# Which projections of a decoder layer run as classical fill and which by seven products: branch B's gates and branch A's u change places

## The chip, the core and the metric

The kernel runs on one core of a Trainium2 chip. Five engines with their own instruction streams share the core's SBUF: TensorE (PE, with its weight loads PEld), VectorE (DVE), ScalarE (ACT), GpSimd (POOL) and SyncE (SP), which here issues most DMA transfers. The metric is the device time of one execution in microseconds (us).

## The reference

Two layers of a decoder trunk on 1024 tokens of width 1024. Each layer projects the normalised input once and feeds three token mixers from slices of the projection:

```python
h = rms_norm(x, g_pre)
p = h @ w_in
(u_a, v_a, gate_a, q_b, k_b, v_b, gate_b, q_c, k_c, v_c, gate_c, merge_logits) = split(p)
y_a = chunk_gmlp(u_a, v_a, gm_w_s, gm_b_s, gm_norm_gain) * silu(gate_a)       # u * (tril(W) LN(v) + b) per 128 tokens
y_b = sliding_window_attention(rope(q_b), rope(k_b), v_b, sinks) * silu(gate_b)  # 8 heads of 64, window 128
y_c = stick_breaking_attention(q_c, k_c, v_c) * silu(gate_c)                    # 4 heads of 128, causal
gates = sigmoid(merge_logits + b_merge)
merged = gates[0] * (y_a @ w_branch_a) + gates[1] * (y_b @ w_branch_b) + gates[2] * (y_c @ w_branch_c)
x = x + rms_norm(merged @ w_out, g_post)
```

All of it is float32. The slices u_a, v_a, gate_a, q_b, gate_b and so on have 512 columns each, k_b and v_b 128, the merge logits 3072.

## The kernel before

**Products in three passes.** Every operand of a matmul is split into a rounded part (`hi`, made by ScalarE) and the rest (`lo`, made by VectorE): `split`, lines 111 and 112. A product is then three matmuls per 128 rows of depth (`mm3`, lines 128 to 130). Since all products go through these helpers, the profile names them by the lines of the helpers and by their tiles.

**Two ways to project.** A slice of the projection is made in one of two ways.
- *Classical fill*: `queue_layer` puts jobs in a queue (`stream`). `proj_t` makes 128 columns with the tokens along the free axis, `proj_n` makes 256 columns with the tokens on partitions. `fill(us)` and `need(label)` take steps of these jobs and put them between the matmuls of the attention branches, so that TensorE has work while other engines make softmaxes. A job's weights are loaded and split one job ahead, into a ring of six tiles (`whi`, `wlo`, `wop`: tag `w`) behind a ring of two raw tiles (`wr`).
- *Seven products*: `dense` takes pairs of 128-column blocks and makes each 2 x 2 block product of halves with seven products in place of eight (Strassen's scheme). It needs sums of quarters of the input, T1, T2, T3 and T4. `Combine` makes these: it loads quarters of the saved input (`hT`), subtracts them on VectorE (lines 694, 698, 700 and 705) and splits them; T1, T2 and T4 take twelve of the 27 SBUF slots (`s0` to `s26`) of 128 x 1024, T3 overwrites half of the input (`place_t3`). `S["T"].go(spare)` does as many of its six steps as free slots allow.

**Order in a layer.** Branch C, branch B, `dense`, `merges`, `project_out`. Branch B works in eight units v, two for each of four query blocks of 128 columns. A unit has `scores` (line 488 on TensorE, then copies and a softmax), two transposes (line 521) and two `attend` (line 545). `scores(v + 2)` is called ahead of unit v's transposes. A query block is projected (`qb`), evacuated by ScalarE (line 279), turned by `rope` (four transfers in SyncE's queue, two passes of GpSimd, lines 293 and 294, one of VectorE, line 295), and split by ScalarE (346) and VectorE (347). Masks of the attention weights are made by GpSimd (line 528).

**The order of the fill around the change** is that of the last line of `queue_layer`: two query blocks, half of v, the other two query blocks, the other half of v, then u. The gates of branch A's first half are fill too; the gates of C and B and the second half of A's gates are pairs of `dense`, as are the merge gates.

**Branch A** is done inside `dense`: statistics of v (lines 617 and 618) and its normalisation (623), the transposed mixing weights (627), and then for each of four groups a product with v and a multiplication with u (640 and 643). The dictionary `then` says behind which pair's third product each piece stands. `gate_task` multiplies one 128-row block of a branch's output with its SiLU gate; the tasks are done at the ends of pairs.

**Who sets the order.** TensorE's order is the one in which the program is written. On the other engines and in the DMA queues a scheduler orders the instructions, and each engine then takes its own in that order.

Of the kernel before, what the change touches and what calls it, by code (L numbers as in the profile page):

```python
# [22 lines left out]
P = 128  # L23
# [4 lines left out]
HT = T // 2  # L28
EPS = 1e-6
NEG = -1e30  # L30
O_UA, O_VA, O_GA = 0, 512, 1024
O_QB, O_KB, O_VB, O_GB = 1536, 2048, 2176, 2304
O_QC, O_KC, O_VC, O_GC = 2816, 3328, 3840, 4352
# [8 lines left out]
def trunk(ctx, tc, x, w_in, gm_w_s, gm_b_s, gm_g, sinks, w_ba, w_bb, w_bc, b_merge, w_out,  # L42
          g_pre, g_post, cos_t, sin_t, out):
    nc = tc.nc
    L = w_in.shape[0]
    x = x.rearrange("b t d -> (b t) d")
    out = out.rearrange("b t d -> (b t) d")
# [12 lines left out]
    def new(dt=F32):  # L60
        i = free.popleft()
        t = sp.tile([P, 1024], dt, name=f"s{i}", tag=f"s{i}", bufs=1)
        held[id(t)] = (i, t)
        return t

    def done(*ts):
        for t in ts:
            free.append(held.pop(id(t))[0])
# [72 lines left out]
    def step():  # L141

        while stream:
            j = stream[0]
            if j.gen is None:
                if j.w is None:
                    j.w = j.load()
                j.gen = j.run(j.w)
                if len(stream) > 1:
                    stream[1].w = stream[1].load()  # L150
            c = next(j.gen, None)
            if c is not None:
                for d in list(deferred):
                    d[0] -= c
                    if d[0] <= 0:
                        deferred.remove(d)
                        d[1]()
                return c
            finished.add(j.label)
            stream.popleft()  # L160
        return None

    def fill(us):
        while us > 0:
            c = step()
            if c is None:
                return
            us -= c

    def need(label):  # L170
        while label not in finished:
            assert step() is not None, label

    def proj_t(label, l, col, evac):

        def run(w):
            wh, wl = w
            for hf in range(2):
                acc = pj()
                for k in range(KD):  # L180
                    mm3(acc, (wh[:, k], wl[:, k]), (h[hf][0][:, k], h[hf][1][:, k]), k == 0, k == KD - 1)
                    if k < KD - 1:
                        yield 0.64
                with tc.high_priority():
                    evac(hf, acc)
                yield 0.64
        stream.append(Job(label, lambda: load_w(w_in[l, :, col:col + P], KD, P), run))
# [57 lines left out]
    def queue_layer(l, S):  # L245
# [104 lines left out]
        def va(j):  # L350
            def ev(pr, acc):
                if j == 0:
                    S["va", pr] = new()
                nc.vector.tensor_copy(S["va", pr].rearrange("p (a b) -> p a b", a=2)[:, :, j * 256:(j + 1) * 256],
                                      acc.rearrange("p (a b) -> p a b", a=2))
            proj_n(f"va{j}", l, O_VA + j * 256, ev)

        def ua(c):
            def ev(hf, acc):
                if hf == 0:  # L360
                    S["ua", c] = new()
                nc.scalar.copy(S["ua", c][:, hf * HT:(hf + 1) * HT], acc)
            proj_t(f"ua{c}", l, O_UA + c * P, ev)
        def qb(hp):
            raw(("qb", hp), O_QB + hp * P, 0.125, lambda: after_q(hp))

        vcj(0); qk(0); qk(1); vcj(1); qk(2); qk(3); gate("a", 0); gate("a", 1)
        raw("kb", O_KB, 1.0, after_k)
        raw("vb", O_VB, 1.0, after_v)
        qb(0); qb(1); va(0); qb(2); qb(3); va(1); ua(0); ua(1); ua(2); ua(3)  # L370

    def branch_c(l, S):
        U = 4 * NB
# [99 lines left out]
    def branch_b(l, S):  # L473
# [86 lines left out]
                nc.sync.dma_start(S["ob"][hp * P:(hp + 1) * P, :], o)  # L560
                done(o)

        need(("qb", 1))
        fill(4)
        ready = {0: scores(0)}
        fill(3)
        ready[1] = scores(1)
# [2 lines left out]
        for v in range(8):  # L570
            if v % 2 == 0:
                o = new()
# [137 lines left out]
    def gate_task(S, br, c):  # L710

        o, g = new(), new()
        nc.sync.dma_start(o, S["o" + br][c * P:(c + 1) * P, :])
        nc.sync.dma_start(g, S["g" + br][c * P:(c + 1) * P, :])
        nc.vector.tensor_tensor(o, o, g, op=ALU.mult)
        nc.scalar.activation(g, g, AF.Sigmoid)
        nc.vector.tensor_tensor(o, o, g, op=ALU.mult)
        nc.sync.dma_start(S["y" + br][c * P:(c + 1) * P, :], o)
        done(o, g)

    def dense(l, S):

        T = S["T"].T
        pairs = [(o + c * P, "g", (br, c)) for o, br, c in ((O_GC, "c", 0), (O_GC, "c", 2), (O_GB, "b", 0), (O_GB, "b", 2),
                                                            (O_GA, "a", 2))]
        pairs += [(O_M + "abc".index(br) * D + dm * P, "m", (i, br, dm)) for i, br in enumerate("cba")
                  for dm in range(0, KD, 2)]

# [76 lines left out]
        a = branch_a(l, S)  # L805
        with tc.issue_after(S["b_act"].ins), tc.issue_after(S["b_dve"].ins):
            next(a)
        tasks = deque([lambda br=br, c=c: gate_task(S, br, c) for br in "cba" for c in range(4)])
        then = {0: lambda: next(a), 1: lambda: (next(a), next(a)), 2: lambda: (next(a), next(a))}
        for p, (col, kind, what) in enumerate(pairs):  # L810
            n = 7 * p
            begin(p + 1)
            u = new()
            out = [new(), new()]
            u2, u3 = u[:, :512], u[:, 512:]
            c11, c12, c21, c22 = (t[:, j * 512:(j + 1) * 512] for t in out for j in range(2))

            def add(o, x, b):
                with tc.high_priority():
                    nc.vector.tensor_tensor(o, x, b, op=ALU.add)  # L820
            p1 = prod(n, "B11")
            if p == len(pairs) - 1:
                S["first"] = load_y(S, "c", True)
            with tc.high_priority():
                nc.scalar.copy(c12, p1)
            add(c11, c12, prod(n + 1, "B21"))
            add(u2, c12, prod(n + 2, "T2"))
            if p in then:
                then[p]()
            add(u3, u2, prod(n + 3, "T3"))  # L830
            p5 = prod(n + 4, "T1")
            add(c22, u3, p5)
            add(u2, u2, p5)
            add(c21, u3, prod(n + 5, "T4"))
            add(c12, u2, prod(n + 6, "B22"))
            done(u)
            for j in range(2):
                if kind == "g":
                    br, c = what
                    nc.sync.dma_start(S["g" + br][(c + j) * P:(c + j + 1) * P, :], out[j])  # L840
                else:
                    i, br, dm = what
                    nc.scalar.activation(out[j], out[j], AF.Sigmoid, bias=bmv(l, "abc".index(br), dm + j))
                    nc.scalar.dma_start(S["sg"][(i * KD + dm + j) * P:(i * KD + dm + j + 1) * P, :], out[j])
            done(*out)
            if p >= 3 and tasks:
                tasks.popleft()()
                if p % 2 and tasks:
                    tasks.popleft()()
        assert not tasks  # L850
        for t in T.values():
            for q in t:
# [232 lines left out]
    with tc.manual_schedule(engines={mybir.EngineType.PE}):  # L1085
# [3 lines left out]
        for l in range(L):  # L1089
            S = states[l]  # L1090
# [49 lines left out]
```

## Time and profile before

| | us |
|---|---|
| median of 3 runs | 2087.54 |
| lowest and highest | 2086.88, 2090.14 |
| the profiled execution | 2087.81 |
| its span, first to last instruction | 2086.1 |
| TensorE busy | 2015.0 |
| VectorE, ScalarE, GpSimd busy | 1218.3, 815.9, 496.5 |

The mean granted clock of TensorE is 0.986 of full speed. Layer 0 takes about the first half of the span. Its branch B runs from 307 us, its seven products from 471 us; those of layer 1 lie about 1031 us later. In the profile `s`, `pj`, `pz`, `ptr` and `pav` are an SBUF slot and the four kinds of PSUM tiles; "a <- b: x, n, m" in a list of waits means that a waited for b, x us in total, n times, the longest m.

### The profile page before, as it was taken

How to read it: one execution, taken by the hardware profiler on the slowest of the kernel's cores; microseconds unless marked ns; L12 is line 12 of the kernel's file. 1: busy time of each engine (PE TensorE's matmuls, PEld its weight loads, DVE VectorE, ACT ScalarE, POOL GpSimd, SP SyncE). 2: the span in 40 equal slices, each digit the busy share in tenths (PEclk: the TensorE clock that was granted, in tenths of full speed). 3: DMA queues.
4: the chain of work that ended last, by engine and by line, in shares of the span. 5: the costliest groups of instructions: out<-in, count | busy, mean ns of one | idle time of the engine just before them, and what ended most of it. 6: DMA issues, size and time to landing. Idle time of an engine off the chain costs nothing.

```text
span 2086.1 us, 26587 instructions
## 1 busy us (share of the span) xinstructions
PE 2015.0 (97%) x10193; PEld 1689.0 (81%) x10193; DVE 1218.3 (58%) x1601; ACT 815.9 (39%) x1485; POOL 496.5 (24%) x501
## 2 busy tenths in 40 slices
PE   7999998998999999999999999989999999999998
PEld 7898887886888888888898888879778888888886
DVE  5555646558776556554546565556677765556533
ACT  6444435543234334213444344445423443432221
POOL 0222222232432230151002221222334222202500
PEclk9999999999999999999999999989999999999999
DMA  7111232123766427633431112222336663376213
GB/s 240 34 41 41 81 82 61 41 73 109 260 235 234 139 80 261 222 133 91 135 129 31 41 41 91 61 61 64 108 129 245 239 214 112 119 254 222 81 51 131
DMA packets 169054, 261.81 MB, mean 126 GB/s; under 512 B 8616, under 2 KB 122336, under 8 KB 168928
## 3 DMA queue, kind: packets, MB, share of 16 engines
q1 hardware_dynamic: 162016, 234.95, 34.3%
q10 hardware_dynamic: 6912, 25.17, 3.0%
q8 instruction: 80, 1.31, 0.3%
q14 instruction: 46, 0.38, 0.1%
HBM read 175.15 MB, written 79.69 MB: 122 GB/s over the span
## 4 chain that ended last, share of the span: by engine, by line
PE 87%; DVE 4%; issue 3%; ACT 2%; POOL 2%; DMA 1%; SPq 0%; POOLq 0%; DVEq 0%; ACTq 0%
PE pj L129 16%; PE pj L128 16%; PE pj L130 16%; PE pz L129 5%; PE pz L130 5%; PE pz L128 5%; PE ptr L129 5%; PE ptr L130 5%; PE ptr L128 5%; PE pz L488 2%; PE ptr L415 1%; PE pav L129 1%; PE pav L545 1%; PE pav L130 1%; POOL s L396 1%
## 5 line engine op out<-in xcount | busy, mean ns | idle before, releaser
L128 PE MATMUL pj<-h,whi 128*128 128x512 f32 x700 | 285.3, 408 | 0.0
L129 PE MATMUL pj<-h,whi 128*128 128x512 f32 x700 | 277.3, 396 | 0.0
L130 PE MATMUL pj<-h,wlo 128*128 128x512 f32 x700 | 276.9, 396 | 0.0
L130 PEld LDWEIGHTS pj<-h,wlo 128*128 128x128 f32 x700 | 131.7, 188 | 31.5
L128 PEld LDWEIGHTS pj<-h,whi 128*128 128x128 f32 x700 | 132.3, 189 | 24.4
L112 DVE TENSOR_TENSOR wlo<-wr,whi 128x1024 fp32r<-128x1024 f32 x80 | 107.0, 1341 | 75.9 <-ACT whi L111 75.5
L129 PEld LDWEIGHTS pj<-h,whi 128*128 128x128 f32 x700 | 132.2, 189 | 22.9
L128 PE MATMUL pj<-whi,h 128*128 128x256 f32 x512 | 149.0, 291 | 1.0 <-ACT h L111 1.0
L111 ACT CAST whi<-wr 128x1024 fp32r<-128x1024 f32 x80 | 84.1, 1051 | 163.0 <-PE pj L129 109.3
L130 PE MATMUL pj<-whi,h 128*128 128x256 f32 x512 | 145.2, 284 | 1.7 <-DVE h L112 1.7
L129 PE MATMUL pj<-wlo,h 128*128 128x256 f32 x512 | 144.8, 283 | 0.0
L111 ACT CAST wop<-s 128x512 fp32r<-128x512 f32 x118 | 73.2, 620 | 183.0 <-PE pz L130 60.7
L111 ACT CAST wop<-wr 128x512 fp32r<-128x512 f32 x120 | 74.4, 620 | 154.2 <-PE ptr L130 38.7
L941 POOL TENSOR_TENSOR s<-s,s 128x512 f32<-128x512 f32 x56 | 81.3, 1455 | 222.1 <-DVE s L935 196.1
L398 DVE TENSOR_TENSOR_SCAN s<-s,ones 128x128 f32<-128x128 f32 (+3 forms) x64 | 87.7, 1370 | 63.7 <-POOL s L393 63.7
L112 DVE TENSOR_TENSOR wop<-wr,wop 128x512 fp32r<-128x512 f32 x120 | 99.8, 836 | 31.9 <-ACT wop L111 31.3
L112 DVE TENSOR_TENSOR wop<-s,wop 128x512 fp32r<-128x512 f32 x118 | 107.3, 909 | 16.3 <-ACT wop L111 16.0
L112 DVE TENSOR_TENSOR s<-ptr,s 128x512 fp32r<-128x512 f32 (+2 forms) x132 | 77.3, 589 | 64.9 <-ACT s L111 64.4
L129 PE MATMUL pj<-h,s 128*128 128x512 f32 x256 | 102.0, 398 | 0.0
L128 PE MATMUL pj<-h,s 128*128 128x512 f32 x256 | 101.2, 395 | 0.0
L130 PE MATMUL pj<-h,s 128*128 128x512 f32 x256 | 100.6, 393 | 0.0
L130 PEld LDWEIGHTS pj<-whi,h 128*128 128x128 f32 x512 | 98.0, 191 | 2.6 <-DVE h L112 2.6
(231 smaller groups left out, 5158.9 us busy)
## 6 DMA issues: line engine op xcount, KB each, us to landing
wr<-in_w_in_dram SPq DMA_DIRECT2D x96, 512.0 KB, 4.2
sg<-s ACTq DMA_DIRECT2D x48, 512.0 KB, 5.0
s<-sg SPq DMA_DIRECT2D x48, 512.0 KB, 5.0
s<-in_w_in_dram SPq DMA_DIRECT2D x28, 512.0 KB, 5.2
s<-in_x_dram SPq DMA_DIRECT2D x16, 512.0 KB, 4.0
hT<-s SPq DMA_DIRECT2D x16, 512.0 KB, 3.4
s<-hT SPq DMA_DIRECT2D x16, 512.0 KB, 4.7
wor<-in_w_out_dram SPq DMA_DIRECT2D x16, 512.0 KB, 3.7
```

The costliest lines, as they stand in the source:

```text
L111: nc.scalar.copy(hi, raw)
L112: nc.vector.tensor_tensor(lo, raw, hi.bitcast(F32), op=ALU.subtract)
L128: nc.tensor.matmul(acc, lh, rh, start=first, stop=False)
L129: nc.tensor.matmul(acc, lh, rl, start=False, stop=False)
L130: nc.tensor.matmul(acc, ll, rh, start=False, stop=last)
L396: nc.gpsimd.affine_select(t2[:, dg], t2[:, dg], pattern=[[-1, P]], compare_op=ALU.is_gt, fill=0.0, base=0, channel_multiplier=1)
L398: nc.vector.tensor_tensor_scan(t1[:, :kl][:, ::-1], t1[:, :kl][:, ::-1], ones.to_broadcast([P, kl]), 1.0, op0=ALU.mult, op1=ALU.mult)
L415: nc.tensor.transpose(pt[:, b - b0], t2[:, b * P:(b + 1) * P], ident)
L488: nc.tensor.matmul(z[:, e * 2 + j], qT[e][:, n * P:(n + 1) * P], kk[i][:, k0:k0 + 256], start=i == 0, stop=i == 1)
L545: nc.tensor.matmul(av[:, j], w, t.rearrange("p (e j) k -> p e j k", j=2)[:, :, j], start=i == 0, stop=i == len(ops) - 1)
L941: eng.tensor_tensor(acc[dm][:, ts], acc[dm][:, ts], sg[:, ts], op=ALU.add)
```

## The change

Three things move. In the fill, the four query blocks come one behind the other, the four gates of branch B follow them, and the two halves of v come last. In `dense`, the two pairs of B's gates are replaced by two pairs of u (kind `"u"`), whose result stays in its SBUF slots for branch A and is not stored; the pieces of branch A move one pair later, and the gate tasks go one to a pair, B's first. Branch B starts when the first query block is there, and with fill of 14 in place of 4. Since u no longer fills four slots during branch B, `Combine` begins its steps earlier. The numbers of lines behind the change are one to three lower.

```diff
--- before.py
+++ after.py
@@ -355,19 +355,17 @@
                                       acc.rearrange("p (a b) -> p a b", a=2))
             proj_n(f"va{j}", l, O_VA + j * 256, ev)
 
-        def ua(c):
-            def ev(hf, acc):
-                if hf == 0:
-                    S["ua", c] = new()
-                nc.scalar.copy(S["ua", c][:, hf * HT:(hf + 1) * HT], acc)
-            proj_t(f"ua{c}", l, O_UA + c * P, ev)
         def qb(hp):
             raw(("qb", hp), O_QB + hp * P, 0.125, lambda: after_q(hp))
 
         vcj(0); qk(0); qk(1); vcj(1); qk(2); qk(3); gate("a", 0); gate("a", 1)
         raw("kb", O_KB, 1.0, after_k)
         raw("vb", O_VB, 1.0, after_v)
-        qb(0); qb(1); va(0); qb(2); qb(3); va(1); ua(0); ua(1); ua(2); ua(3)
+        for i in range(4):
+            qb(i)
+        for i in range(4):
+            gate("b", i)
+        va(0); va(1)
 
     def branch_c(l, S):
         U = 4 * NB
@@ -560,8 +558,8 @@
                 nc.sync.dma_start(S["ob"][hp * P:(hp + 1) * P, :], o)
                 done(o)
 
-        need(("qb", 1))
-        fill(4)
+        need(("qb", 0))
+        fill(14)
         ready = {0: scores(0)}
         fill(3)
         ready[1] = scores(1)
@@ -721,8 +719,8 @@
     def dense(l, S):
 
         T = S["T"].T
-        pairs = [(o + c * P, "g", (br, c)) for o, br, c in ((O_GC, "c", 0), (O_GC, "c", 2), (O_GB, "b", 0), (O_GB, "b", 2),
-                                                            (O_GA, "a", 2))]
+        pairs = [(O_GC, "g", ("c", 0)), (O_UA, "u", 0), (O_UA + 2 * P, "u", 2), (O_GC + 2 * P, "g", ("c", 2)),
+                 (O_GA + 2 * P, "g", ("a", 2))]
         pairs += [(O_M + "abc".index(br) * D + dm * P, "m", (i, br, dm)) for i, br in enumerate("cba")
                   for dm in range(0, KD, 2)]
 
@@ -805,8 +803,8 @@
         a = branch_a(l, S)
         with tc.issue_after(S["b_act"].ins), tc.issue_after(S["b_dve"].ins):
             next(a)
-        tasks = deque([lambda br=br, c=c: gate_task(S, br, c) for br in "cba" for c in range(4)])
-        then = {0: lambda: next(a), 1: lambda: (next(a), next(a)), 2: lambda: (next(a), next(a))}
+        tasks = deque([lambda br=br, c=c: gate_task(S, br, c) for br in "bca" for c in range(4)])
+        then = {1: lambda: next(a), 2: lambda: (next(a), next(a)), 3: lambda: (next(a), next(a))}
         for p, (col, kind, what) in enumerate(pairs):
             n = 7 * p
             begin(p + 1)
@@ -835,18 +833,19 @@
             add(c12, u2, prod(n + 6, "B22"))
             done(u)
             for j in range(2):
-                if kind == "g":
+                if kind == "u":
+                    S["ua", what + j] = out[j]
+                elif kind == "g":
                     br, c = what
                     nc.sync.dma_start(S["g" + br][(c + j) * P:(c + j + 1) * P, :], out[j])
                 else:
                     i, br, dm = what
                     nc.scalar.activation(out[j], out[j], AF.Sigmoid, bias=bmv(l, "abc".index(br), dm + j))
                     nc.scalar.dma_start(S["sg"][(i * KD + dm + j) * P:(i * KD + dm + j + 1) * P, :], out[j])
-            done(*out)
+            if kind != "u":
+                done(*out)
             if p >= 3 and tasks:
                 tasks.popleft()()
-                if p % 2 and tasks:
-                    tasks.popleft()()
         assert not tasks
         for t in T.values():
             for q in t:
```

VectorE's order around query block 2 of layer 0, whose slots are `s13_3297` (evacuated block) and `s11`, `s18` (split) before, `s23_2905` and `s7`, `s2` after. Before:

```order
L295 TENSOR_TENSOR s13_3297<-s13_3297,s21_3336 128x1024
L347 TENSOR_TENSOR s11_3344<-s13_3297,s11_3344 64x1024
L347 TENSOR_TENSOR s18_3345<-s13_3297,s18_3345 64x1024
L498 COPY_PREDICATED s24_3415<-mprev_79,pz_3416 128x2x128
L501 COPY_PREDICATED s24_3415<-mprev_79,pz_3431 128x512
L505 TENSOR_REDUCE mx_3442<-s24_3415 128x8
L506 SCALAR_TENSOR_TENSOR mx_3442<-mx_3442,nsnk8_82 128x8
L507 TENSOR_TENSOR es_3444<-mx_3442,snk8_81 128x8
```

The rotation's last pass and the two splits stand directly ahead of the scores that use them (`pz_3416`, unit 4). After:

```order
L504 SCALAR_TENSOR_TENSOR mx_3032<-mx_3032,nsnk8_82 128x8
L505 TENSOR_TENSOR es_3034<-mx_3032,snk8_81 128x8
L295 TENSOR_TENSOR s23_2905<-s23_2905,s5_2974 128x1024
L112 TENSOR_TENSOR s9_3076<-ptr_3071,s9_3076 128x512
L509 TENSOR_TENSOR ls_2944<-ls_2944,es_2945 128x8
L510 RECIPROCAL ls_2944<-ls_2944 128x8
L511 TENSOR_TENSOR s24_2920<-s24_2920,ls_2944 128x1024
L112 TENSOR_TENSOR s21_3096<-ptr_3091,s21_3096 128x512
L347 TENSOR_TENSOR s7_2982<-s23_2905,s7_2982 64x1024
L347 TENSOR_TENSOR s2_2983<-s23_2905,s2_2983 64x1024
L554 TENSOR_TENSOR s0_3004<-pav_3129,s23_3136 64x256
```

They now stand among the softmaxes of units 1 and 2; the same scores come some 25 rows further down.

VectorE's order at the split of the second half of v's last weights (`wlo_3370` before, `wlo_3734` after). Before:

```order
L694 TENSOR_TENSOR s26_4140<-s19_4138,s26_4140 128x1024
L112 TENSOR_TENSOR s0_3308<-ptr_3303,s0_3308 128x512
L511 TENSOR_TENSOR ls_3251<-ls_3251,es_3252 128x8
L512 RECIPROCAL ls_3251<-ls_3251 128x8
L513 TENSOR_TENSOR s16_3227<-s16_3227,ls_3251 128x1024
L112 TENSOR_TENSOR wlo_3370<-wr_3367,whi_3369 128x1024
L112 TENSOR_TENSOR s9_3355<-ptr_3350,s9_3355 128x512
```

After:

```order
L703 TENSOR_TENSOR s13_4067<-s13_4067,s26_4059 128x1024
L112 TENSOR_TENSOR s16_3978<-ptr_3973,s16_3978 128x512
L354 COPY s23_3999<-pj_3928 128x2x256
L510 RECIPROCAL ls_3880<-ls_3880 128x8
L112 TENSOR_TENSOR s19_4056<-s10_4052,s12_4055 128x1024
L554 TENSOR_TENSOR s2_3653<-pav_4011,s7_4020 64x256
L511 TENSOR_TENSOR s11_3856<-s11_3856,ls_3880 128x1024
L554 TENSOR_TENSOR s2_3653<-pav_4011,s7_4020 64x256
L112 TENSOR_TENSOR s15_4064<-s26_4059,s25_4063 128x1024
L112 TENSOR_TENSOR s9_4071<-s13_4067,s21_4070 128x1024
L112 TENSOR_TENSOR wlo_3734<-wr_3731,whi_3733 128x1024
L354 COPY s10_4098<-pj_4001 128x2x256
```

Before, one subtraction of T and a softmax stood near it. Now subtractions and splits of T's first half (`s10`, `s26`, `s13` and their `lo` tiles) and the softmax of the last unit stand ahead of it.

VectorE's order at the start of the seven products, from the last attention sums (L556 before, L554 after) on. Before, with `s8_4416` the second half's T1, `s12_4423` its T2, `s14_4431` its T4 and `s23`, `s5`, `s22`, `s1` the tiles of v:

```order
L617 BN_STATS st_4462<-s5_3027 128x6
L694 TENSOR_TENSOR s8_4416<-s10_4414,s8_4416 128x1024
L618 BN_AGGR mv_4454<-st_4462 128x2
L617 BN_STATS st_4465<-s5_3027 128x6
L617 BN_STATS st_4468<-s22_3135 128x6
L112 TENSOR_TENSOR s26_4420<-s8_4416,s21_4419 128x1024
L618 BN_AGGR mv_4454<-st_4465 128x2
L618 BN_AGGR mv_4454<-st_4468 128x2
L112 TENSOR_TENSOR wop_4500<-wr_4389,wop_4500 128x512
L617 BN_STATS st_4471<-s22_3135 128x6
L617 BN_STATS st_4474<-s1_3209 128x6
L698 TENSOR_TENSOR s10_4414<-s12_4423,s10_4414 128x1024
```

After, with `s13_4418` the second half's T2, `s2_4426` its T4:

```order
L696 TENSOR_TENSOR s22_4074<-s13_4418,s22_4074 128x1024
L554 TENSOR_TENSOR s8_4049<-pav_4383,s17_4392 64x256
L698 TENSOR_TENSOR s13_4418<-s13_4418,s18_4076 128x1024
L354 COPY s10_4098<-pj_4335 128x2x256
L554 TENSOR_TENSOR s8_4049<-pav_4383,s17_4392 64x256
L112 TENSOR_TENSOR wop_4412<-wr_4398,wop_4412 128x512
L112 TENSOR_TENSOR wop_4415<-s11_4408,wop_4415 128x512
L112 TENSOR_TENSOR s26_4423<-s13_4418,s16_4422 128x1024
L703 TENSOR_TENSOR s2_4426<-s2_4426,s13_4418 128x1024
L112 TENSOR_TENSOR h11_75<-s5_4050,h10_74 128x1024
L818 TENSOR_TENSOR s14_4499<-s14_4499,pz_4525 128x512
L112 TENSOR_TENSOR s17_4430<-s2_4426,s0_4429 128x1024
```

Before, the statistics of v (BN_STATS) run between the steps of T. After, the remaining steps of T come first, between them the last copy of v (L354), and the statistics follow.

## The prediction

> **What bounds the kernel now.** I read the page first, then the list of what TensorE waits for, then the stretches around its longest waits, then the chain and the rows of single engines there.
>
> ```profile
> span 2086.1 us, 26587 instructions
> PE 2015.0 (97%) x10193; PEld 1689.0 (81%) x10193; DVE 1218.3 (58%) x1601; ACT 815.9 (39%) x1485; POOL 496.5 (24%) x501
> ```
>
> TensorE is busy for 97% of the span, and the change keeps its number of matmuls: in each layer four projections leave the seven-product form and four enter it. So only its 71 us of idle time, and the matmuls that run at half clock behind a wait, can move. Its waits by cause (total us, times, longest):
>
> ```profile
> PE pz L488 <- DVE s L347: 16.2, 4, 7.7
> ...
> PE pz L488 <- DVE s L501: 7.8, 2, 3.9
> PE pj L128 <- ACT s L111: 7.4, 1, 7.4
> PE ptr L128 <- ACT s L111: 6.4, 1, 6.4
> ...
> PE ptr L521 <- DVE s L556: 3.2, 2, 1.6
> ```
>
> L488 is the score matmul of branch B; its largest wait is for L347, the split of a rotated query block. L128 is in the seven products, where operands of T come late. The stretches of these waits, beside one without any (columns: the stretch, its length, then busy us of TensorE, weight loads, VectorE, ScalarE, GpSimd, then granted clock, DMA share, GB/s):
>
> ```profile
> 310.00:330.00 20.00, 16.09 (x113) 15.88 (x113) 15.28 (x22) 11.39 (x39) 4.25 (x3) 0.83 0.01 2
> 355.00:375.00 20.00, 11.93 (x53) 9.96 (x52) 7.69 (x10) 4.87 (x9) 6.42 (x5) 0.74 0.21 52
> 465.00:490.00 25.00, 15.57 (x66) 12.25 (x67) 23.93 (x35) 11.99 (x17) 4.95 (x5) 0.86 0.39 127
> 600.00:800.00 200.00, 200.00 (x859) 160.94 (x858) 120.60 (x161) 80.64 (x113) 54.58 (x40) 1.00 0.46 160
> ```
>
> At 355 us nobody is busy: a chain of latencies. At 465 us VectorE is full (23.93 of 25): a queue. In the seven products proper (600 to 800) TensorE never idles.
>
> **Part 1, query blocks in a row.** The chain ahead of the wait that ends at 369 us (start, length, what):
>
> ```profile
> 354.26 0.60 ACT s L279
> ...
> 356.74 2.37 DMA s<-s
> ...
> 361.60 2.35 POOL s L294
> 363.97 1.24 DVE s L295
> ...
> 365.88 0.94 ACT s L346
> 366.84 1.22 DVE s L347
> ...
> 369.36 3.36 PE pz L488 x14
> ...
> 373.15 0.43 PE pj L129
> ...
> 407.00 1.91 PE pz L488 x16
> ```
>
> From the evacuation of query block 2 to the use of its split pass 369.4 - 354.3 = 15.1 us, and scores(4) stands close behind that projection. TensorE idles 8.1 us per layer (16.2 in all). Behind it 14 matmuls take 3.36 us where 16 take 1.91, so 1.7 us more, and three more take 0.43 us where 0.23 is the full rate (2.80 us for the twelve of a product, below): 0.6. Together 16.2 + 2 x 2.3 = 20.8 us. In the changed order block 2 is projected ahead of scores(2), and between its last matmul and scores(4) lie some 120 matmuls of 512 columns (28 us) and 7 us of scores, transposes and attention. That is more than 15.1, so the term goes whole: **-20.8**. Block 3 has still more room, some 55 us.
>
> What moves with it: per layer eight transfers in SyncE's queue, four GpSimd and six VectorE passes now run among the first softmaxes. The wait on L501 (3.9 us: the score buffers of block 0 are drained behind a softmax) keeps its price. TensorE comes to scores(2) 12.1 us behind scores(0), before 11.8; ScalarE gets two copies of 0.6 us there, but the path is VectorE's: **0**, bounds -1 to +1 per layer. The wait of 1.6 us on L556 may return in another place: in ScalarE's order block 3's split stands ahead of the first gate half's evacuation, which so comes 15 to 16 us behind block 3's last matmul, while TensorE asks for that accumulator after 14.7. I take 1.1 us in place of 1.6: **-0.5** per layer, bounds -1.6 to +1.
>
> **Part 2, v last.** va(1) follows va(0) directly, and the second half of its weights takes buffers that va(0) frees only 3.6 us before TensorE needs them. In VectorE's order seven 1024-wide passes of T and a softmax pass stand between scores(7) and that split. Rows of such passes (start, length, engine, line):
>
> ```profile
> 485.83 1.21 DVE L705 TENSOR_TENSOR s<-s,s 128x1024 f32<-128x1024 f32 x1
> 486.97 1.21 DVE L112 TENSOR_TENSOR s<-s,s 128x1024 fp32r<-128x1024 f32 x1
> 488.10 0.68 DVE L617 BATCH_NORM_STATS2 st<-s 128x6 f32<-128x512 f32 x1
> 488.70 1.20 DVE L112 TENSOR_TENSOR s<-s,s 128x1024 fp32r<-128x1024 f32 x1
> ...
> 495.97 4.36 DVE L623 TENSOR_SCALAR s<-s,mv,rs 128x512 f32<-128x512 f32 x5
> ...
> 501.45 1.45 DVE L623 TENSOR_SCALAR s<-s,mv,rs 128x512 f32<-128x512 f32 x3
> ...
> 505.22 0.67 DVE L820 TENSOR_TENSOR s<-s,ptr 128x512 f32<-128x512 f32 x1
> 505.82 2.38 DVE L112 TENSOR_TENSOR wop<-wr,wop 128x512 fp32r<-128x512 f32 x3
> ```
>
> Starts lie 1.14 us apart behind a 1024-wide pass and 0.60 behind a 512-wide one. And a transfer of hT, issued and landed:
>
> ```profile
> 469.87 0.87 SPq L683 DMA_DIRECT2D s<-hT  x2
> ```
>
> ```profile
> 470.33 4.09 DMA s<-hT
> ```
>
> From issue to landing are 470.33 + 4.09 - 469.87 = 4.5 us. The last transfer of T's first half takes the slot that scores(7) gives back. From its landing VectorE has nine wide passes (10.3 us: seven of T, the softmax, the weights' split), three of 512 (1.8) and under 2 us of small rows, 14.0 in all, so it ends 18.6 us behind scores(7). TensorE asks after 17.7: a wait of 0.9. GpSimd's masks fall into the same time:
>
> ```profile
> 312.31 1.55 DVE L506 SCALAR_TENSOR_TENSOR mx<-mx,nsnk 128x8 f32<-128x8 f32 x1
> ...
> 326.19 0.16 DVE L506 SCALAR_TENSOR_TENSOR mx<-mx,nsnk 128x8 f32<-128x8 f32 x1
> ```
>
> ```profile
> 311.44 2.40 POOL L294 TENSOR_TENSOR s<-s,s 128x1024 f32<-128x1024 f32 x1
> ...
> 418.17 0.65 POOL L528 TENSOR_SCALAR_AFFINE_SELECT s<-s 128x512 fp32r<-128x512 f32 x1 [1.38 <-ACT s L111]
> ```
>
> The 128x8 row took 1.55 us beside a GpSimd pass, until that ended at 313.84, and 0.16 without one. Four masks of 0.65 lie in the window and can hold VectorE for 2.6 us: the wait is 0.9 to 3.5. I take 2, about the middle, since the masks themselves wait for VectorE in part: **+2** per layer.
>
> [...]
>
> **Part 3, start of the seven products.** TensorE there (start, length of one matmul, wait):
>
> ```profile
> 471.34 0.40 PE L128 MATMUL ptr<-h,wop 128*128 128x512 f32 x1
> ...
> 474.14 0.40 PE L128 MATMUL pz<-h,wop 128*128 128x512 f32 x1
> ...
> 478.11 0.40 PE L130 MATMUL pj<-s,wop 128*128 128x512 f32 x1
> 485.90 0.80 PE L128 MATMUL pj<-s,wop 128*128 128x512 f32 x1 [7.39 <-ACT s L111]
> 488.23 0.79 PE L129 MATMUL pj<-s,wop 128*128 128x512 f32 x1 [1.53 <-DVE s L112]
> ...
> 493.07 0.40 PE L129 MATMUL ptr<-h,wop 128*128 128x512 f32 x1
> ```
>
> A product takes 2.80 us. From 478.35 to 493.07 only ten matmuls and four transposes pass (2.8 us at full rate): 14.7 - 2.8 = 11.9 us are lost. Layer 1 waits 1 us less (6.4 for 7.4), so 23 in all.
>
> After the change the first half of T and the first step of the second are done in branch B. But VectorE's backlog hardly shrinks: seven wide passes of T remain where eight did, and the eight statistics (L617) and normalisations (L623) of v still follow. The last transfer but one takes a slot that is given back 5.3 us ahead of the first product (its start is t) and lands at t - 0.6. From there to the split of the second pair's second operand stand 7 x 1.14 + 15 x 0.60 + 8 x 0.60 us, 1.9 of small rows, and the L623 rows: 5.7 as here, 3.7 if all go like the last three (0.46 each). That is 27.4 to 29.4, and 1.7 in which VectorE waits for products: it ends at about t + 29.4. TensorE would ask at t + 8 x 2.80 + 0.5 = 22.9. So 6.5 us are lost, in four waits of 0.7, 0.8, 2.6 and 2.4. The gain is 11.5 - 6.5 = 5.0 per layer, **-10**. Bounds of the loss per layer: 0 (as at 600 to 800) and 11.9 (as now).
>
> What a wait of 2.6 us costs in clock no row shows. Behind 1.6 us nothing is lost; behind 3.9 us the clock of 0.83 over 20 us means 6.8 us at half rate. 2.6 is nearer to 1.6: **0**, upper end 2.3 per wait as at 369 us. [...]
>
> **At no cost.** The u pairs do the adds of the gate pairs that they replace, less four stores. The gates' evacuation (four copies each on ScalarE and VectorE per layer, 0.6 us) replaces eight of u on ScalarE; SyncE's queue gets four stores in branch B and loses four later. The gate tasks, now one per pair up to pair 14, hide under VectorE's 80 idle of 200 us; if the last came late, merging would wait for one load, about 5 us. In SyncE's queue a load of pair 3 stands ahead of those of pair 1 and waits until T3 is placed; pair 1's load still lands about 4 us before its use, and costs what exceeds that.
>
> **Sum.** -20.8 - 1.0 + 4.0 - 10.0 = -27.8 against the profiled execution's 2087.8 (span 2086.1; 0.3 over the median 2087.54): **2060**.
>
> **Rivals.**
> - *The products' start keeps its loss.* VectorE's 23.93 of 25 speaks for it, against it that the late transfers are gone. With 11.9 us lost there and va(1) waiting the full 3.5: 2087.8 - 20.8 - 1 + 7 = 2073; as a case 2068 to 2078. 0.23.
> - *That start becomes clean,* since statistics run only where TensorE has its operands: 2087.8 - 20.8 - 1 + 4 - 23 = 2047; 2040 to 2052. Against it stand the 29 us of rows. 0.13.
> - *The queries were not the limit:* the wait for block 2 returns as a longer one on L501, as its rotation now shares VectorE and ScalarE with the first softmaxes. It takes 12 to 16 us there per layer to cancel the gain; the added rows are about 6 us, most of them behind L501. 2084 to 2092, 0.04.
> - *Slower:* va(1)'s split. T's passes in branch B stretch until TensorE waits 16 us there (the 2 counted and half of 27.8): that cancels the gain, and at 20 us it is 2060 + 2 x 18 = 2096. VectorE's 14 us of rows would have to double, and 2.6 us of masks don't do that alone. 0.05.
> - The forecast, 2052 to 2068: 0.55.
>
> The range 2046 to 2074 leaves out the last two rivals and the outer parts of the first two. A measurement of this kernel can tell about 0.2%, 4.2 us, from no change: 0.04 for that, slower 0.05, faster 0.91.
>
> **What would show it.** Right: no wait of the score matmul (now L486) on L347; TensorE full where scores(4) is; a short wait of an L129 matmul on a weight split some 25 us ahead of the products; in their first two pairs several waits under 3 us on L112 and none of 7; VectorE full for 30 us there. Wrong: L486 waiting longer on L499, more than 4 us on the weight split, or half clock in the first two pairs.

## The result, and the profile after

The changed kernel takes 2069.68 us (median; 2067.85 to 2070.14), the kernel before, on the same chip, 2087.21: a ratio of 0.9912, 95% interval 0.9895 to 0.9929. The forecast was 2060, with a range of 2046 to 2074. So the sign and the range held, and some 10 us of the expected 27.8 did not come. The page of the changed kernel:

```profile
span 2068.4 us, 26597 instructions
PE 2015.1 (97%) x10193; PEld 1688.1 (82%) x10193; DVE 1227.0 (59%) x1609; ACT 808.3 (39%) x1477; POOL 504.3 (24%) x501
```

TensorE is as busy as before (2015.1 us) in a span that is 17.7 us shorter: only idle time went. What it waits for now (us in total, times, the longest):

```profile
PE pj L128 <- ACT s L257: 9.2, 2, 4.9
...
PE pz L486 <- DVE s L499: 8.1, 2, 4.1
...
PE ptr L130 <- DVE wop L112: 5.3, 2, 3.0
PE pj L130 <- DVE wop L112: 2.9, 2, 2.4
PE pz L130 <- DVE wop L112: 2.7, 2, 2.2
```

The 16.2 us of the score matmul's wait for L347 are gone, and the 7.4 and 6.4 us in the seven products have become waits of up to 3.0 us. On top stands a line that the list of before did not have: TensorE waits for L257, ScalarE's evacuation of a gate, 9.2 us in all. The stretches of these waits in layer 0 (columns as in the prediction):

```profile
310.00:330.00 20.00, 15.94 (x73) 13.52 (x72) 16.10 (x18) 11.78 (x33) 7.75 (x5) 0.83 0.21 55
355.00:375.00 20.00, 16.67 (x78) 14.16 (x79) 10.14 (x15) 6.82 (x15) 1.68 (x3) 0.83 0.16 52
465.00:490.00 25.00, 22.31 (x94) 17.49 (x93) 21.99 (x40) 8.46 (x14) 1.29 (x1) 0.94 0.43 136
600.00:800.00 200.00, 200.00 (x859) 160.96 (x858) 126.43 (x163) 82.61 (x118) 50.26 (x37) 1.00 0.53 175
```

From 310 to 330 TensorE's busy time and clock are as before. At 355 TensorE works 16.67 of 20 us where it had 11.93, but the granted clock is 0.83 and not 1.00 (before, 0.74): a new wait sits at the old place. From 465 to 490 its busy time rose from 15.57 to 22.31.

The new wait in TensorE's order (start, length of one matmul, wait):

```profile
353.56 0.40 PE L130 MATMUL pj<-h,wlo 128*128 128x512 f32 x1
358.33 0.80 PE L128 MATMUL pj<-h,whi 128*128 128x512 f32 x1 [4.37 <-ACT s L257]
358.92 0.63 PE L129 MATMUL pj<-h,whi 128*128 128x512 f32 x1
...
364.04 0.44 PE L130 MATMUL pj<-h,wlo 128*128 128x512 f32 x1
364.33 0.40 PE L128 MATMUL pj<-h,whi 128*128 128x512 f32 x1
```

A projection has two accumulators (`pj`). The second gate's first half needs the one that holds the first gate's first half, and that is still full. Up to 364 us the matmuls then run at half rate (0.43 us apart at a granted clock of 0.50, 0.23 apart at 1.00 from there on): 5.7 us long, so 2.9 lost beside the 4.4. ScalarE and VectorE there:

```profile
339.01 0.58 ACT L279 ACTIVATE s<-pj 128x512 f32<-128x512 f32 x1
...
354.88 1.04 ACT L346 CAST s<-s 64x1024 fp32r<-64x1024 f32 x1
...
357.69 0.59 ACT L257 COPY s<-pj 128x512 f32<-128x512 f32 x1 [0.70 <-DVE s L347]
```

```profile
347.35 1.97 DVE L504 SCALAR_TENSOR_TENSOR mx<-mx,nsnk 128x8 f32<-128x8 f32 x1
...
354.73 1.22 DVE L347 TENSOR_TENSOR s<-s,s 64x1024 fp32r<-64x1024 f32 x1
...
356.44 1.22 DVE L347 TENSOR_TENSOR s<-s,s 64x1024 fp32r<-64x1024 f32 x1
```

Block 3 is evacuated at 339.0 (L279), and its rotated tile is split until 357.66. At 357.69 the gate's copy starts, and its releaser is that split. A copy out of PSUM has nothing to do with a split of another projection, unless it writes where the split still reads.

### The profile page after: what moved, and what is told of

Read it like the earlier page. It is cut to its first block, busy times and chain, and to the rows that moved or that the text cites. A ratio compares the mean times of both kernels' runs of the same rounds, so it can differ in the third digit from the quotient of the medians.

```text
span 2068.4 us, 26597 instructions
## 1 busy us (share of the span) xinstructions
PE 2015.1 (97%) x10193; PEld 1688.1 (82%) x10193; DVE 1227.0 (59%) x1609; ACT 808.3 (39%) x1477; POOL 504.3 (24%) x501
## 4 chain that ended last, share of the span: by engine, by line
PE 87%; DVE 6%; ACT 3%; issue 2%; POOL 1%; DMA 1%; SPq 0%; DVEq 0%; POOLq 0%; ACTq 0%
PE pj L130 16%; PE pj L129 16%; PE pj L128 16%; PE pz L130 6%; PE pz L128 5%; PE pz L129 5%; PE ptr L130 5%; PE ptr L128 5%; PE ptr L129 5%; PE ptr L413 1%; PE pz L486 1%; PE pav L543 1%; PE pav L129 1%; DVE s L112 1%; PE pav L130 1%
## 5 line engine op out<-in xcount | busy, mean ns | idle before, releaser
L112 DVE TENSOR_TENSOR wop<-s,wop 128x512 fp32r<-128x512 f32 x118 | 97.8, 834 | 12.2 <-ACT wop L111 11.8
```

The source lines that it names most:

```text
L112: nc.vector.tensor_tensor(lo, raw, hi.bitcast(F32), op=ALU.subtract)
```

## The experiments

Twelve kernels were run. All times below are medians, each with its ratio to runs of the kernel before on the same chip and the 95% interval of that ratio.

**The two halves of the change alone.** `e1_queries_only` is the kernel before with the query blocks in a row and the matching start of branch B. `e2_exchange_only` is the changed kernel with the order and the start of before:

```diff
# e1, on before
-        qb(0); qb(1); va(0); qb(2); qb(3); va(1); ua(0); ua(1); ua(2); ua(3)
+        qb(0); qb(1); qb(2); qb(3); va(0); va(1); ua(0); ua(1); ua(2); ua(3)
-        need(("qb", 1)); fill(4)
+        need(("qb", 0)); fill(14)
# e2, on after
-        qb(0); qb(1); qb(2); qb(3); gate b 0 to 3; va(0); va(1)
+        qb(0); qb(1); va(0); qb(2); qb(3); va(1); gate b 0 to 3
-        need(("qb", 0)); fill(14)
+        need(("qb", 1)); fill(4)
```

> The kernel before with one part of the change: the four query blocks in a row, then both halves of v, then u as fill; branch B starts at the first block; the seven products are those of before. Theory 1 (the wait of scores(4) was the limit of branch B, and what the change then lost there is the evacuation of the first gate half behind block 3's rotation): no wait on L347, and since v's first half, evacuated by VectorE, follows block 3, no wait of 4 us there; start of the products as before, 11 to 12 us lost per layer: 2087 - 21 = 2066, 2063 to 2070. Rival (the rotations among the first softmaxes cost what they save, whatever the fill behind them): a wait of 3 to 5 us behind block 3 all the same, 2073 to 2080.

> The other part alone: branch B's gates as fill and u by seven products, gate tasks and branch A as in the change, but the query blocks in the order of before (v's halves between them, gates last, start at the second block with fill of 4). Theory 1: the wait on L347 stays (16 us in both layers), the start of the products gets better by 3 to 6 us per layer, since T begins early and v's statistics need not wait for the end of the fill: 2075 to 2082. Rival (T's earlier start gains nothing, VectorE's backlog is what it was): 2085 to 2089.

e1: 2078.77 us, 0.9955 (0.994 to 0.997). e2: 2076.56 us, 0.9944 (0.9929 to 0.9959). Against 2088.44 these are gains of 9.7 and 11.9, 21.6 together, where the whole change gained 17.5: the parts are not quite separate, some 4 us are lost when they meet. e2 came as its theory said; e1 came in the range of its rival. The waits of e1 from 290 to 560 us:

```profile
PE pj L128 <- ACT s L111: 7.8, 1, 7.8
PE pj L128 <- DVE s L354: 5.7, 1, 5.7
PE pz L488 <- DVE s L501: 4.1, 1, 4.1
```

The products' start keeps its 7.8 us without the exchange. And the new wait is there without it too, for whatever follows block 3 in the fill, here the first half of v (L354, evacuated by VectorE). So it comes from the query blocks in a row, and it ate half of their gain. In e2 the wait for L347 is back (16.2 us in all), there is no wait behind block 3, and the waits at the products' start are at most 2.3 us.

**What stands behind block 3, and GpSimd's share.** `e3_v_between` puts v's first half between block 3 and the gates. `e6_rope_dve` gives the two rotation passes of blocks 2 and 3 to VectorE:

```diff
# e3, on after
         for i in range(4):
             qb(i)
+        va(0)
         for i in range(4):
             gate("b", i)
-        va(0); va(1)
+        va(1)
# e6, on after, for hp >= 2
-            nc.gpsimd.tensor_tensor(sw, sw, S["sin"], op=ALU.mult)
-            nc.gpsimd.tensor_tensor(t, t, S["cos"], op=ALU.mult)
+            nc.vector.tensor_tensor(sw, sw, S["sin"], op=ALU.mult)
+            nc.vector.tensor_tensor(t, t, S["cos"], op=ALU.mult)
```

> The changed kernel with v's first half moved between the query blocks and the gates (blocks 0 to 3, v first half, four gates, v second half). Theory 1 (the 4.4 us wait and its half clock come from the first gate half's evacuation, which in ScalarE's order and by its SBUF slot stands behind block 3's split): the wait goes, 7 us per layer: 2070 - 14 = 2056, 2053 to 2060. Rival (VectorE is late there as a whole, held by GpSimd): a wait of 2 us or more appears at the copies of v or at the transposes, 2062 to 2070.

> The changed kernel, with the two multiplications of the rotation of query blocks 2 and 3 on VectorE in place of GpSimd. Theory 2 (a GpSimd pass holds VectorE's short softmax rows, 1.8 to 2.2 us each, and so makes the gate's evacuation late): those rows fall to 0.2 us, the wait of 4.4 us falls below 2: 2056 to 2063. Rival (only the length of the chain and its place in ScalarE's order count; VectorE gets 4.9 us more work per layer): the wait stays above 3 us, 2067 to 2073.

e3: 2070.05 us, 0.9914 (0.9899 to 0.9929). e6: 2068.57 us, 0.9902 (0.9886 to 0.9919). Neither differs from the changed kernel by more than the runs scatter. The theory of e3 fell: the wait moves to VectorE's copy of v and grows:

```profile
PE pj L128 <- DVE s L354: 5.3, 1, 5.3
```

In the changed kernel the short softmax row takes 1.97 us (above) and ends at 349.32, beside a GpSimd pass that runs from 346.90 to 349.29. In e6 it takes 0.59 us, and the wait stays:

```profile
350.90 0.59 DVE L505 SCALAR_TENSOR_TENSOR mx<-mx,nsnk 128x8 f32<-128x8 f32 x1
```

```profile
PE pj L128 <- DVE s L253: 5.1, 1, 5.1
```

In e6 block 3's second split ends at 357.86, as late as in the changed kernel, and both copies of the gate stand behind it (VectorE's at 358.10, ScalarE's at 358.59). So the engine that evacuates is not the cause, and taking GpSimd's passes away does not help. By itself e6 does not clear GpSimd, since it gives VectorE more work in the same place; e8 below leaves GpSimd's passes where they are, and there the wait goes.

**The buffer.** The SBUF slots come from a list, first in, first out, in the order of the program. There, block 3's raw tile is given back as soon as its rotation and splits have been written down; that is early in the program and late in time. By the time of the first evacuation behind block 3 the slots ahead of it have been handed out, and that evacuation takes this very slot (`s22` in the changed kernel and in e3). It has to wait for the split that reads the slot, with eight others behind it on the list. `e8_slot_later` gives this one tile back some 20 us of fill later; the gate then takes `s9`. `e4_stats_early` tests the other cost, the products' start: v's statistics are issued when va(1) is evacuated. `e9_slot_and_stats` has both.

```diff
# e8, in after_q(hp)
-            done(t)
+            if hp == 3:
+                deferred.append([20.0, lambda: done(t)])
+            else:
+                done(t)
# e4, in the evacuation of va(1), and no more in branch_a
+                for a in range(2):
+                    nc.vector.bn_stats(st, S["va", pr] ... [:, a])
+                    nc.vector.bn_aggr(S["mv"][:, pr * 2 + a], st)
```

> The changed kernel with the buffer of query block 3's raw tile given back to the list some 20 us of fill later, so that the first gate's tile takes a buffer that has long been free. Theory (the buffer: the list hands out buffers in the order of the program, in which block 3's raw tile is given back before its rotation and its second split have run; the first gate half's evacuation writes into that very buffer and can't start before the split's last row at 357.66): the evacuation comes when its matmuls end, the wait of 4.37 us on L128 and the half rate of some 5.6 us behind it are gone, 6 to 7 us per layer, 2055 to 2059 us. Rival (ScalarE's and VectorE's queues: the splits and the exponentials of two softmaxes stand ahead of the evacuation whatever buffer it writes): the wait stays at 3 us or more, 2066 to 2071.

> The changed kernel with the statistics of v (L615 and L616, 16 short rows) issued as va(1) is evacuated, inside branch B, and not at the start of the seven products. Theory (VectorE is the late one there: its statistics and normalisations stand ahead of the u's second halves, so PE waits 2.24 and 2.37 us and runs at half rate for 3.4 us after each): some 5.6 us of VectorE leave that place, both waits fall below 1 us and their half rate goes with them, 3 to 4 us per layer, 2061 to 2064 us. Rival (VectorE is held there by the transfer of hT, for which L696 waits, or by the hold of its short rows beside GpSimd): the waits stay within 0.5 us of 2.2 and 2.4, 2068 to 2071. The wait of 4.4 us at the first gate half stays under both.

> Both edits at once: block 3's buffer given back later, and the statistics of v issued inside branch B. If the two costs are separate, the gains add: 2049 to 2055 us by the theories of both, no waits above 1 us left at the first gate half and at the products' start. If VectorE is what both lack (the 16 statistics rows take the room in branch B in which the waits shrank), the sum comes short by 3 us or more, and the wait for L499 (4.1 us per layer) grows.

e8: 2054.14 us, 0.9844 (0.983 to 0.9857). e4: 2067.89 us, 0.9908 (0.9895 to 0.9922). e9: 2051.46 us, 0.9831 (0.9817 to 0.9844).

In e8 the gate's copy stands among the exponentials, 6.7 us earlier, and TensorE goes through (ScalarE, then TensorE):

```profile
350.91 0.19 ACT L510 ACTIVATION_READ_ACCUMULATOR s<-s,mx 128x1 f32 x1
351.01 0.56 ACT L257 COPY s<-pj 128x512 f32<-128x512 f32 x1
351.47 0.41 ACT L510 ACTIVATE s<-s,mx 128x128 f32<-128x128 f32 x1
```

```profile
353.56 0.40 PE L130 MATMUL pj<-h,wlo 128*128 128x512 f32 x1
353.99 0.66 PE L522 MATMUL ptr<-ident,s 128*128 128x128 f32 x4
354.40 0.48 PE L128 MATMUL pj<-h,whi 128*128 128x512 f32 x1
```

That is 15.5 us for the time at which one buffer is given back, with no work added or taken away, a little more than the theory's range. The two waits (9.2 us) and the half rate behind them (5.1, worked out below) make 14.3 of it, and the waits at the products' start did not shrink (11.9 us for 10.9): the theory of the buffer is shown. ScalarE's order is part of the mechanism, not a rival of it, since the scheduler puts the copy ahead of the exponentials once its slot is free.

e4 gains at most 2 us. The two waits merge into one of 3.4 us, and ScalarE's row there names most of the reason:

```profile
484.69 0.62 ACT L111 CAST wop<-wr 128x512 fp32r<-128x512 f32 x1 [8.99 <-DMA wr<-in_w_in_dram]
```

With the statistics gone, the split waits for the weights of the second pair (the cast ends at 485.31, and a normalisation on VectorE holds the split until 486.69). Besides, the wait on L257 in layer 0 is 6.3 us here, and in e15 below, where it was 4.4: at branch B's start full rate is back before 328 us and not at 330 (the matmuls are 0.23 us apart from 327.88 in e4 and 327.39 in e15, from 330.04 in the changed kernel), so TensorE comes to that wait sooner (1.25 us in e15). e9 is only 2.7 us faster than e8, and for the same reason: a wait of 3.3 us stays at the products' start, where its expectation had none above 1. That its time lies in the range of the added gains says little, since e8 alone lies in it. Each pair's two raw tiles are the whole ring `wr`, so the second pair's loads wait until the first pair's have been split: in the changed kernel they are issued at 478.18 and 486.17, right behind splits that end at 478.03 and 486.11.

**The second pair's loads.** `e11_pair1_slots` is e8 with the raw weights of the second pair in two free slots, as later odd pairs have them. `e15_pair1_alone` is the changed kernel with that alone, `e12_pair1_slots_stats` is e11 with the early statistics.

```diff
-                    if p % 2 and p > 2:
+                    if p % 2:
```

> The kernel of e8 (block 3's buffer given back later; 2054.1 us) with the raw weights of the second pair of products in two of the free buffers, so that both raw weight buffers are free for the third pair at once; nothing else moves. Theory (the third pair's load is what the waits at the products' start end on: it is issued at 478.18 in the changed kernel, behind the last split of the second pair's raw tile, and lands at 481.9): the load is issued some 10 us earlier, ScalarE's wait of 9.3 us for it goes, and of the waits of 2.2 and 3.3 us with the half rate behind them 3 to 6 us per layer go, 2043 to 2049 us. Rival (VectorE's queue: statistics and normalisations stand ahead of the splits, whenever the weights land): waits within 0.5 us of e8's, 2052 to 2056.

> The changed kernel with the second pair's raw weights in free buffers alone; the first gate's evacuation keeps its buffer and its wait of 4.4 us. Theory (the two costs are separate and the loads end the second wait): of the waits of 2.24 and 2.37 us one goes with its half rate, 2 to 4 us per layer, 2061 to 2066 us. Rival (in the changed kernel both waits end on VectorE's queue alone, ScalarE's split having been done 2 to 3 us earlier): 2067 to 2071.

> The kernel of e11 (block 3's buffer given back later, the second pair's raw weights in free buffers; 2048.1 us) with the statistics of v in branch B. In e11 PE still waits 2.25 us for a split that stands behind the statistics on VectorE, and its weights have landed long before. Theory (VectorE's order is now the last that holds it): that wait falls below 1 us in both layers, 2043 to 2046 us. Rival (e13 went back to 2066 with these statistics and more fill: the room they take in branch B delays T or other splits): a wait of 3 us or more returns at the products' start, 2050 to 2066.

e11: 2048.08 us, 0.9811 (0.9796 to 0.9825), the fastest of all. e15: 2062.5 us, 0.9877 (0.9862 to 0.9893). e12: 2053.03 us, 0.9837 (0.9823 to 0.9851). (What the first of these expectations calls the third pair is the second.) The second pair's two loads in e8 and, below, in e11:

```profile
470.81 0.38 SPq L781 DMA_DIRECT2D wr<-in_w_in_dram  x1
478.81 0.37 SPq L781 DMA_DIRECT2D wr<-in_w_in_dram  x1
```

```profile
444.60 0.46 SPq L781 DMA_DIRECT2D s<-in_w_in_dram  x1
456.84 0.61 SPq L781 DMA_DIRECT2D s<-in_w_in_dram  x1
```

They leave 26 and 22 us earlier, the wait of 3.3 us in e8 goes, and 6 us are gained, as both theories said, with the slot given back later or without it (e15 against the changed kernel: 7). The rest of the waits of e11 from 290 to 520 us:

```profile
PE pz L489 <- DVE s L502: 4.1, 1, 4.1
PE ptr L130 <- DVE wop L112: 2.2, 1, 2.2
PE ptr L129 <- DVE h L112: 1.4, 1, 1.4
PE pz L130 <- DVE wop L112: 0.5, 1, 0.5
```

The theory of e12 fell: with the statistics out of the way, waits for T3 (`h`) and for a split take their place, and it is 5 us slower than e11. The edit makes VectorE's work no less; it only changes which operand comes late.

```profile
PE ptr L129 <- DVE h L112: 3.4, 2, 2.3
PE pj L130 <- DVE wop L112: 2.4, 1, 2.4
```

**More cover at branch B's start.** `e14_fill` is e8 with `FB` beginning with 9 in place of 4, so 5 us more fill between the second and third set of scores. `e13_all` has all four edits.

> The kernel of e8 with 9 us of fill in place of 4 between the second and the third set of scores at branch B's start. Theory (TensorE waits 4.1 us per layer for L502's row there, since VectorE's copies for the second set come late, and runs at half rate behind it): 5 us of matmuls cover the wait, 4 us and some 3 of half rate per layer, against 5 us of cover less at branch B's end, where VectorE is 82% busy: 2042 to 2050 us. Rival (the cover is only moved: the end of branch B waits for what it lost): 2051 to 2056, new waits of 2 us or more on pav or ptr after 400.

> All four edits: block 3's buffer given back later, the statistics in branch B, the second pair's weights in free buffers, and 9 us of fill. If the gains add: 2032 to 2042 us. If VectorE's total work at the seam of branch B and the products bounds them together: within 3 us of the better of the other two.

e14: 2054.72 us, 0.9844 (0.9829 to 0.9859). e13: 2066.31 us, 0.9898 (0.9881 to 0.9914). The wait on L502 goes, and two others take its place in e14:

```profile
PE ptr L522 <- DVE s L557: 4.3, 1, 4.3
PE pav L546 <- POOL s L529: 3.9, 2, 3.2
```

The first ends at 353 us, the second at 462, near branch B's end; in exchange the waits for `wop` at the products' start are gone. The cover was only moved, and nothing is gained, as the rival said. e13 has these two waits and one of 3.3 us (4.0 in layer 1) for `wop` besides: its waits are some 12 us longer than e11's over both layers, and its mean granted clock is 0.990 where e11's is 0.998. Why the edits bring this together, when the statistics alone cost 5 us and the fill alone nothing, is not settled.

## Why the prediction was right, and where it was off

*Part 1, the queries:* right. The wait for L347 is gone from both layers, and with it its half rate: -20.8 as forecast; e2, which takes the row away, has it back with 16.2 us. e8, which has the row and no wait behind block 3, lies 1.0% of 2087, some 21 us, below e2. The wait on L499 is 8.1 us for 7.8, within the bounds.

*The mis-sized term:* "I take 1.1 us in place of 1.6", the first gate half's evacuation. It measured 4.4 and 4.9 us, and half-rate stretches of 5.7 and 4.4 us cost half their length on top. With 3.2 us gone that is 9.2 + 5.1 - 3.2 = +11.1 in place of -1.0, far past the bound of +1 per layer. The prediction had the place, the accumulator and the split ahead of it in ScalarE's order. Two things failed. The chain from block 3's last matmul to the copy took 357.69 - 338.8 = 18.9 us and not 15 to 16, and no price for the clock was set on this wait. The reason behind the order, the slot, was not seen at all, and so neither was that giving one slot back later takes the whole wait away (e8).

*Part 2, v last:* the wait on va(1)'s split came to some 0.2 us in either layer, 0.4 in place of +4, and that narrowly. The split (second line) ends at 439.40, and the matmul that needs it starts right behind:

```profile
428.87 3.21 POOL L526 TENSOR_SCALAR_AFFINE_SELECT s<-s 128x512 fp32r<-128x512 f32 x2 [0.30 <-ACT s L507]
```

```profile
438.18 1.22 DVE L112 TENSOR_TENSOR wlo<-wr,whi 128x1024 fp32r<-128x1024 f32 x1
```

```profile
439.11 0.28 PE L128 MATMUL pj<-whi,h 128*128 128x256 f32 x1
439.45 0.39 PE L129 MATMUL pj<-wlo,h 128*128 128x256 f32 x1
```

The chain without the masks, which gave 0.9, was near. What failed is the hold by the masks: VectorE's 1024-wide passes beside them (from 428.72 and 430.37) took 1.22 us each, as elsewhere, and it was the masks that took longer, two of them 3.21 us where the one at 432.26 took 0.64.

*Part 3, the products' start:* the count of waits was nearly right and the clock wrong. Forecast were waits of 0.7, 0.8, 2.6 and 2.4, measured are 0.45, 2.24 and 2.37 in layer 0 and 0.55, 2.24 and 3.02 in layer 1. But the 0 for the clock behind a wait of 2.6 us failed:

```profile
486.17 0.50 PE L130 MATMUL ptr<-h,wop 128*128 128x512 f32 x1 [2.24 <-DVE wop L112]
...
487.34 0.63 PE L128 MATMUL ptr<-h,wop 128*128 128x512 f32 x1
...
490.32 0.45 PE L129 MATMUL pz<-h,wop 128*128 128x512 f32 x1
...
495.94 0.49 PE L130 MATMUL pj<-h,wop 128*128 128x512 f32 x1 [2.37 <-DVE wop L112]
```

At 487.04, 0.9 us behind the first wait's end, the matmuls go to half rate for 3.4 us (granted clock 0.50 up to 490.45). Behind the second wait they do so 1.33 us after its end (0.50 from 497.27), and behind the two long waits of layer 1 nearly at once (0.50 from 1507.62 and 1517.86, waits that end at 1507.52 and 1517.95). Over both layers the loss is 10.9 us of waits and 6.7 of half rate, 17.6 for 23: -5.4 in place of -10. What ends the waits was half seen. In the changed kernel both end on VectorE's queue, as forecast: the first split stands behind the statistics, the second (495.21) behind 4.5 us of normalisations. "Pair 1's load still lands about 4 us before its use" came out nearly, too: the second load has landed at 489.94, and TensorE asks for its operand at 493.57. What was missed is that an earlier load lets the scheduler put that split ahead of the normalisations (at 488.85 in e15), and e4, e11 and e15 show what this is worth.

*The sum:* -20.8 + 11.1 + 0.4 - 5.4 + 0.3 = -14.4; the spans differ by 17.7. A wait of 0.6 us per layer at the end of branch B that is gone too makes 1.2 of that difference; 2.1 us I can't place.

That the range held is in part luck. The mis-sized term (12.1 us off) and part 3 (4.6 off) alone would have brought 2077, outside it; part 2 (3.6 the other way) and 3.3 us that the sum did not hold brought the time back. The band given to the forecast itself, 2052 to 2068, was missed by 1.7 us. The time lies in the band of the rival by which the products' start keeps its loss: three quarters of that loss did stay (17.6 of 23), but va(1), which that rival has waiting, hardly waited, and the new wait behind block 3 is not in it.

## What to carry to other kernels

When a change frees a wait by moving work earlier, look at what the next instruction writes into, not only at what it reads: a first-in-first-out list of buffers goes by the order of the program, and can hand out one whose last reader has yet to run, with others behind it on the list. Price a wait of TensorE of 2.2 us and more, as here, with the half rate that may follow: in the changed kernel it cost 11.8 us beside 20.1 us of waits (behind block 3 and at the products' start). And a step that is moved off one queue gains only until the next operand is late (e4, e12, e14): ask for the loads behind it first.

## What the runs showed of the hardware

The drop to half rate does not go by the length of a wait alone. In e8 the same wait of 2.23 us stands in both layers; in layer 0 full rate follows, in layer 1 half rate:

```profile
478.80 0.50 PE L130 MATMUL ptr<-h,wop 128*128 128x512 f32 x1 [2.23 <-DVE wop L112]
479.14 0.39 PE L128 MATMUL ptr<-h,wop 128*128 128x512 f32 x1
```

```profile
1491.68 0.50 PE L130 MATMUL pz<-h,wop 128*128 128x512 f32 x1 [2.23 <-DVE wop L112]
...
1492.29 0.63 PE L129 MATMUL pz<-h,wop 128*128 128x512 f32 x1
1492.72 0.63 PE L130 MATMUL pz<-h,wop 128*128 128x512 f32 x1
```

In the changed kernel the granted clock is 0.50 from 357.32 to 364.15, from 487.03 to 490.44 and from 497.27 to 500.68 us, and in layer 1 from 1507.62 to 1511.03, among others. These stretches are 3.41 us long, or twice that, and their ends lie 126.29, 10.24 and 1010.35 us apart. These are 37, 3 and 296 times 3.413 us, the length estimated from the 10.24 us. In e8 the half rate ends at 492.11 and 1495.63, 294 times 3.413 apart.

The stretches of 3.413 us between and around these times can be read one by one. The wait of 4.37 us behind block 3 leaves 3.36 us of idle time in the one from 353.91, at a clock of 1.00, and 1.01 in the next, and the clock is 0.50 in that one and in the one behind it. The stretch from 483.62 has 2.24 us of idle time at 1.00, the next is at 0.50 without idle time, the one behind it at 1.00. In the kernel before, 1.62 us in the stretch from 394.04 cost no clock: it is 1.00 there and in the next. Of the 2.23 us in layer 0 of e8, 1.88 lie in one stretch and 0.35 in the next, and full rate follows; in layer 1 all 2.23 lie in one, and half rate follows.

Where the rate before and behind can be read, the least idle time in a stretch at full rate that half rate followed is 1.92 us (e9, ahead of 478.68), the most that full rate followed 1.89 (e8, ahead of 478.80, with 0.01 between matmuls). A stretch at half rate was followed by another with 0.59 us of idle time (e6, ahead of 1518.31), and by full rate with 0.09 (the changed kernel, from 1517.86). The idle time is counted from the modelled ends of the matmuls, and no run shifted a wait against these stretches on purpose, so the figures of e6, e8 and e9 are estimates from the starts and lengths of their matmuls, and not tested.
